# The softmax of the attention given an earlier place in the schedule of a hybrid decoder layer

## The chip, the core and the metric

The kernel runs on one core of a Trainium2 chip. The core has five instruction queues that matter here: TensorE (PE), VectorE (DVE), ScalarE (ACT), GpSimd (POOL) and SyncE (SP), which issues transfers. Each takes its instructions in a fixed order, and an instruction that waits holds all behind it. Times are microseconds on the device, from the start of the program to its end; the median of several runs is the number that counts.

## The reference

The program computes one layer of a decoder on 16 learned tokens and 1024 tokens of width 1024, in 32-bit floats:

```python
u = rmsnorm(h, norm1_w)
rq, rk, rv, rg, dq, dk, dv, gates = split(u @ w_in)
ro = (silu(rg) * group_norm(retention(rope(rq), rope(rk), rv))) @ w_ret_o
dq, dk = rope(rmsnorm(dq)), rope(rmsnorm(dk))
p = softmax(where(mask, q @ k.T / 8, -1e30))     # two maps for each of 8 heads
do = rmsnorm((p[0] - lam * p[1]) @ v) * (1 - lam_init) @ w_diff_o
h = h + (sigmoid(g_ret) * ro + sigmoid(g_diff) * do) @ w_out
a, b = split(causal_dwconv(rmsnorm(h) @ w_up))
out = h + (silu(a) * b) @ w_down
```

The part that the change touches is `p`: the two softmaxes of a head, and their difference with the weight lam.

## The kernel before

Every 32-bit matrix is split into a high part (a cast to fp32r) and a low part (the remainder), and a product is three matmuls: high by high, high by low, low by high. PE therefore streams some 15,000 matmuls, and the other engines cast, subtract, empty the banks and do the rest.

Phase 1 makes the projections of `u` and, among them, the eight heads of attention. `projections` is a generator that gives out half a product (12 matmuls of 342 to 348 columns) at a time; `attention` is another, and `blend` runs the two in turn, 58 units of projection to a head. The finished products go to `evacuate`: for dq and dk it squares them on ACT (L303), splits the squares in sqh (ACT, L241) and sql (DVE, L246), rotates the product on DVE and POOL (L570 to L573), and a little later PE sums the squares by a matmul into the bank `st`. For rq and rk the rotation is L550 to L555, on DVE and POOL as well; for others DVE multiplies once (L606). POOL also computes the low part of the weights (L229).

In `attention`, a block of 128 queries goes through `scores` for both maps. PE makes the scores of a piece of keys into one of four banks `sc` (L175); DVE adds the mask and takes the row's minimum (L686; the scores come negated, so their minimum is the largest logit), which empties the bank; with more than one piece DVE joins the minima (L692); ACT takes the exponential and its sum (L693). When both maps are there, DVE takes the reciprocals (L697) and a product (L698), ACT scales the second map (L699), and DVE adds it to the first (L700). PE then transposes the result (`turn`, L709), ACT and DVE split it in ah and al (L241, L246), and PE multiplies it with the values into the bank `ot`.

The order of the instructions on each engine is fixed when the program is built: outside of a few parts that are ordered by hand, a scheduler takes the instructions by priority, which is their place in the program's text unless something else is said, and by what it estimates to be ready. Tiles come from pools with a few buffers each: two banks `acc` for products, four `sc`, one `st`, one `ot`.

The second to fourth phases (retention, the output products, the MLP) follow and don't call `scores`.

Of the kernel before, what the change touches and what calls it, by code (L numbers as in the profile page):

```python
# [13 lines left out]
AF = mybir.ActivationFunctionType  # L14
ALU = mybir.AluOpType
AX = mybir.AxisListType
# [81 lines left out]
class Builder:  # L98
# [562 lines left out]
    def attention(self, h):  # L661
        V, A, G, E, S = self.V, self.A, self.G, self.E, self.S
# [7 lines left out]
        def scores(t0, m, n, pieces):  # L670

            sm = self.tmp("sm", n=16, bufs=4)
            s = []
            for c in range(2):
                sc_ = self.big() if m > 2 else self.tmp("hs", n=16)
                for i, (a0, sz) in enumerate(pieces):
                    ps = self.sc()
                    self.mm(ps[:m, :sz], QA[c][:, t0:t0 + m], K[c][:, a0:a0 + sz], True, False)
                    self.mm(ps[:m, :sz], QB[c][:, t0:t0 + m], K[c][:, a0:a0 + sz], False, True)
                    if m == 2:  # L680
                        mk = self.hm[:m, :sz]
                    elif i == len(pieces) - 1:
                        mk = self.mask[:, 584 - sz:584]
                    else:
                        mk = self.mask[:, :sz]
                    V.tensor_tensor_reduce(out=sc_[:m, a0:a0 + sz], in0=ps[:m, :sz], in1=mk, scale=1.0, scalar=3e38,  # L686
                                           op0=ALU.add, op1=ALU.min, accum_out=sm[:m, 4 * c + i:4 * c + i + 1])
                np_ = len(pieces)
                mx = sm[:m, 4 * c:4 * c + 1]
                if np_ > 1:  # L690
                    mx = sm[:m, 4 * c + 3:4 * c + 4]
                    V.tensor_reduce(out=mx, in_=sm[:m, 4 * c:4 * c + np_], axis=AX.X, op=ALU.min)  # L692
                A.activation(sc_[:m, :n], sc_[:m, :n], AF.Exp, bias=mx, scale=-1.0,  # L693
                             accum_out=sm[:m, 10 + c:11 + c])
                s.append(sc_)
                yield 0.2 + n / 1000
            V.reciprocal(sm[:m, 12:14], sm[:m, 10:12])  # L697
            V.tensor_mul(sm[:m, 13:14], sm[:m, 13:14], self.nlam[:m])  # L698
            A.activation(s[1][:m, :n], s[1][:m, :n], AF.Copy, scale=sm[:m, 13:14])  # L699
            V.scalar_tensor_tensor(out=s[0][:m, :n], in0=s[0][:m, :n], scalar=sm[:m, 12:13], in1=s[1][:m, :n],  # L700
                                   op0=ALU.mult, op1=ALU.add)
            return s[0]

        def turn(pieces, meta=None):
# [18 lines left out]
        def rows(c):  # L723
            n = NMETA + P * (c + 1)
            k = -(-n // 512)
            sz = [2 * (n // (2 * k))] * k
            sz[0] += n - sum(sz)
            return (yield from scores(NMETA + P * c, P, n, [(sum(sz[:i]), sz[i]) for i in range(k)]))
# [3 lines left out]
        self.spill["do", h] = d, db  # L732
        outs = [(14, 258), (272, 256), (528, 256), (784, 256)]
        halo = yield from scores(HALO, 2, NMETA, [(0, NMETA)])
        ahead = yield from rows(0)

# [4 lines left out]
        for b in range(2):  # L741
            ps = self.tr()
# [5 lines left out]
        ps = self.tr()  # L748
# [4 lines left out]
        for p in range(4):  # L753
# [31 lines left out]
            for jj in range(p + 1):  # L785
# [4 lines left out]
                for kk in range(2):  # L790
                    j = 2 * jj + kk
                    lo = 128 if last and kk == 1 else 0
                    out = ot[:, o0 + lo:nq]
# [6 lines left out]
            t0, n = outs[p]  # L800
# [506 lines left out]
```

## Time and profile before

| | us |
|---|---|
| median of three runs | 2567.45 (2563.02 to 2570.38) |
| profiled execution | 2568.86 |
| its span on the core | 2567.1 |
| TensorE busy | 2509.6 (98%) |
| VectorE busy | 1550.9 (60%) |
| ScalarE busy | 904.0 (35%) |
| GpSimd busy | 816.8 (32%) |

A matmul overlaps the one ahead of it, so busy time of PE is no measure of how fast it goes; the time between the starts of two matmuls is, and where PE idles the trace names the instruction that released it. The granted clock of TensorE is given as a share of 2.4 GHz; half of that, 1.2 GHz, is its other level, and a mean between the two is a stretch in which both occurred. Attention runs from about 100 to 1190 us.

### The profile page before, as it was taken

The page shows a single profiled execution, that of the slowest core. Times are in us where ns is not written, and L with a number is a line of the kernel's source. Part 1 is how long each engine was busy: PE and PEld are TensorE (multiplying, and loading weights), DVE is VectorE, ACT ScalarE, POOL GpSimd, SP SyncE. Part 2 cuts the span into 40 slices and gives each one's busy share as a digit, 9 for nine tenths or more (in the row PEclk, how much of TensorE's full clock was granted, in tenths as well). Part 3 has the DMA queues.
Part 4 walks back from the last instruction along what each step waited for, and adds up shares of the span by engine and source line. Part 5 has one row for each costly group of instructions (what it writes and reads, how often), then busy time and mean ns, then how long its engine had stood idle before and what let it go on. Part 6 is the DMA issues. An engine that isn't in the chain of part 4 may idle for free. (4 is left out here: it accounts for less than half of the span.)

```text
span 2567.1 us, 40420 instructions
## 1 busy us (share of the span) xinstructions
PE 2509.6 (98%) x15444; PEld 2416.9 (94%) x15444; DVE 1550.9 (60%) x3228; ACT 904.0 (35%) x1881; POOL 816.8 (32%) x649
## 2 busy tenths in 40 slices
PE   8999999999999999999999999999999999999999
PEld 8899998999999999999998899999999999999998
DVE  7665757556463737453787887652555566555555
ACT  5343444444343525333466553332311111111111
POOL 1424343322222222222333332434332333333232
PEclk9999999999999999999999999999999999999999
DMA  4524242323324242423443434522111111111112
GB/s 165 129 84 108 63 115 71 107 76 93 104 81 120 62 121 65 117 84 104 116 107 90 105 99 134 185 93 99 38 50 46 50 50 41 50 50 42 50 50 87
DMA packets 171538, 224.55 MB, mean 87 GB/s; under 512 B 26712, under 2 KB 109264, under 8 KB 171344
## 3 DMA queue, kind: packets, MB, share of 16 engines
q1 hardware_dynamic: 165440, 202.70, 26.1%
q0 software_dynamic: 5760, 19.17, 3.5%
q8 instruction: 121, 1.98, 0.3%
q14 instruction: 73, 0.60, 0.1%
q10 hardware_dynamic: 144, 0.10, 0.0%
HBM read 160.20 MB, written 42.35 MB: 79 GB/s over the span
## 5 line engine op out<-in xcount | busy, mean ns | idle before, releaser
L175 PE MATMUL acc<-b,wh 128*128 128x342 f32 (+3 forms) x5948 | 1451.0, 326 | 15.7 <-DVE b L429 9.2
L175 PEld LDWEIGHTS acc<-b,wh 128*128 128x128 f32 x5948 | 1033.7, 190 | 28.4 <-issue 9.2
L175 PE MATMUL acc<-b,wl 128*128 128x342 f32 (+3 forms) x2974 | 966.9, 325 | 1.5 <-POOL wl L229 1.5
L229 POOL TENSOR_TENSOR wl<-wr,wh 128x512 fp32r<-128x512 f32 x366 | 507.6, 1404 | 1148.8 <-ACT wh L228 1136.5
L175 PE MATMUL sc<-b,wh 128*128 128x342 f32 (+2 forms) x2580 | 648.6, 334 | 1.1 <-ACT b L241 1.1
L175 PEld LDWEIGHTS acc<-b,wl 128*128 128x128 f32 x2974 | 564.1, 190 | 7.7 <-POOL wl L229 2.6
L175 PEld LDWEIGHTS sc<-b,wh 128*128 128x128 f32 x2580 | 455.2, 189 | 22.5 <-ACT b L241 1.3
L175 PE MATMUL sc<-b,wl 128*128 128x342 f32 (+2 forms) x1290 | 429.3, 334 | 0.0
L228 ACT CAST wh<-wr 128x512 fp32r<-128x512 f32 x366 | 212.8, 618 | 574.9 <-issue 241.2
L175 PEld LDWEIGHTS sc<-b,wl 128*128 128x128 f32 x1290 | 243.8, 189 | 10.0
L246 POOL TENSOR_TENSOR b<-b,b 128x512 fp32r<-128x512 f32 (+1 forms) x86 | 138.3, 1608 | 304.9 <-ACT b L241 262.7
L606 DVE TENSOR_TENSOR ev<-acc,b 128x342 f32<-128x342 f32 (+1 forms) x144 | 74.0, 514 | 187.7 <-PE acc L175 184.1
L241 ACT CAST b<-b 128x512 fp32r<-128x512 f32 (+3 forms) x137 | 102.1, 750 | 214.0 <-DVE b L1242 145.6
L693 ACT ACTIVATE b<-b,sm 128x272 f32<-128x272 f32 (+7 forms) x128 | 101.0, 789 | 150.4 <-DVE sm L692 118.6
L1205 DVE SCALAR_TENSOR_TENSOR b<-b,cols,b 128x1024 f32<-128x1024 f32 x88 | 148.8, 1691 | 2.3
L686 DVE CUSTOM_DVE_ANT_0 b<-sc,consts 128x144 f32<-128x144 f32 (+6 forms) x224 | 106.6, 503 | 39.3 <-PE sc L175 38.6
L1196 DVE TENSOR_TENSOR b<-sc,b 128x342 f32<-128x342 f32 x84 | 42.5, 511 | 139.4 <-PE sc L175 139.4
L246 DVE TENSOR_TENSOR al<-sc,ah 128x512 fp32r<-128x512 f32 (+2 forms) x144 | 77.6, 539 | 68.3 <-ACT ah L241 68.0
L241 ACT CAST ah<-sc 128x512 fp32r<-128x512 f32 (+2 forms) x144 | 67.3, 467 | 121.8 <-PE sc L709 84.0
L1220 DVE TENSOR_TENSOR b<-b,sc 128x512 f32<-128x512 f32 x117 | 78.7, 683 | 48.8 <-PE sc L175 48.8
L175 PE MATMUL sc<-b,b 128*128 128x264 f32 (+9 forms) x480 | 96.8, 319 | 1.9 <-DVE sm L686 1.9
L1203 DVE TENSOR_SCALAR b<-b,cols 128x1024 f32<-128x1024 f32 x44 | 81.5, 1853 | 1.6
(248 smaller groups left out, 2665.4 us busy)
## 6 DMA issues: line engine op xcount, KB each, us to landing
wr<-w_in SPq DMA_DIRECT2D x170, 256.0 KB
wr<-w_up SPq DMA_DIRECT2D x88, 256.0 KB
d<-ev SPq DMA_DIRECT2D x120, 171.0 KB
b<-b POOLq DMA_DIRECT2D x72, 260.0 KB, 4.6
b<-d SPq DMA_DIRECT2D x256, 64.0 KB
b<-d SPq DMA_DIRECT2D x24, 513.0 KB
wr<-w_down SPq DMA_DIRECT2D x44, 256.0 KB
b<-d SPq DMA_DIRECT2D x32, 260.0 KB
```

Source lines behind the costliest of these rows:

```text
L175: self.E.matmul(out, lhsT=l, rhs=r, start=start, stop=stop)
L228: self.A.copy(h, raw)
L229: (self.G if el == "G" else self.V).tensor_sub(l, raw, h.bitcast(F32))
L241: self.A.copy(dh, src)
L246: (self.V if el == "V" else self.G).tensor_sub(dl, src, dh.bitcast(F32))
L606: V.tensor_mul(o[:, :n], ps[:, :n], self.rb[:, cs])
L686: V.tensor_tensor_reduce(out=sc_[:m, a0:a0 + sz], in0=ps[:m, :sz], in1=mk, scale=1.0, scalar=3e38, op0=ALU.add, op1=ALU.min, accum_out=sm[ ...
L693: A.activation(sc_[:m, :n], sc_[:m, :n], AF.Exp, bias=mx, scale=-1.0, accum_out=sm[:m, 10 + c:11 + c])
L1196: self.V.tensor_mul(up[:, t0:t0 + n], ps[:, :n], self.rb2[:, t0:t0 + n])
L1203: V.tensor_scalar(out=o[:, q], in0=up[:, q], scalar1=self.cw(2, fi), scalar2=self.cb(fi), op0=ALU.mult, op1=ALU.add)
L1205: V.scalar_tensor_tensor(out=o[:, q], in0=up[:, NMETA - 2 + i:T - 2 + i], scalar=self.cw(i, fi), in1=o[:, q], op0=ALU.mult, op1=ALU.add)
L1220: self.V.tensor_add(h, h, ps)
```

## The change

The change puts the operations of `scores` on DVE and ACT under a raised priority: the scheduler takes them as if they stood 300 instructions earlier in the program. No instruction is added, removed or altered. The core of the diff, whose other part puts L692 and L693 under the same line:

```diff
-                    V.tensor_tensor_reduce(out=sc_[:m, a0:a0 + sz], in0=ps[:m, :sz], in1=mk, scale=1.0, scalar=3e38,
-                                           op0=ALU.add, op1=ALU.min, accum_out=sm[:m, 4 * c + i:4 * c + i + 1])
+                    with self.tc.high_priority(offset=300):
+                        V.tensor_tensor_reduce(out=sc_[:m, a0:a0 + sz], in0=ps[:m, :sz], in1=mk, scale=1.0, scalar=3e38,
+                                               op0=ALU.add, op1=ALU.min, accum_out=sm[:m, 4 * c + i:4 * c + i + 1])
...
-            V.reciprocal(sm[:m, 12:14], sm[:m, 10:12])
-            V.tensor_mul(sm[:m, 13:14], sm[:m, 13:14], self.nlam[:m])
-            A.activation(s[1][:m, :n], s[1][:m, :n], AF.Copy, scale=sm[:m, 13:14])
-            V.scalar_tensor_tensor(out=s[0][:m, :n], in0=s[0][:m, :n], scalar=sm[:m, 12:13], in1=s[1][:m, :n],
-                                   op0=ALU.mult, op1=ALU.add)
+            with self.tc.high_priority(offset=300):
+                V.reciprocal(sm[:m, 12:14], sm[:m, 10:12])
+                V.tensor_mul(sm[:m, 13:14], sm[:m, 13:14], self.nlam[:m])
+                A.activation(s[1][:m, :n], s[1][:m, :n], AF.Copy, scale=sm[:m, 13:14])
+                V.scalar_tensor_tensor(out=s[0][:m, :n], in0=s[0][:m, :n], scalar=sm[:m, 12:13], in1=s[1][:m, :n],
+                                       op0=ALU.mult, op1=ALU.add)
```

The lines behind move down by one to three: L686 becomes L687, L692 L694, L697 L700, L698 L701, L700 L703 in the order of the changed kernel. The text goes on by the names of before.

On DVE, in the first block of head 0 (about 125 us in the trace of before), this stood in a row; sh_1193 is the rotated half of a projection, sql_1189 the low half of its squares, sm_1168 the minima and sums of the block, b_1169 its result, b_1235 the next block's scores:

```order
L570 STREAM_SHUFFLE sh_1193<-b_1058 128x346
L246 TENSOR_TENSOR sql_1189<-sq_1187,sqh_1188 128x346
L571 TENSOR_TENSOR b_1058<-b_1058,b_125 128x346
L697 RECIPROCAL sm_1168<-sm_1168 128x2
L573 TENSOR_TENSOR b_1058<-b_1058,sh_1193 128x346
L698 TENSOR_TENSOR sm_1168<-sm_1168,nl 128x1
L686 ISA b_1235,sm_1234<-sc_1236,consts 128x400
L686 ISA sm_1234 128x1
L700 SCALAR_TENSOR_TENSOR b_1169<-b_1169,sm_1168,b_1201 128x272
```

In the changed kernel this stands in its place, on the same engine:

```order
L570 STREAM_SHUFFLE sh_1193<-b_1058 128x346
L700 RECIPROCAL sm_1168<-sm_1168 128x2
L571 TENSOR_TENSOR b_1058<-b_1058,b_125 128x346
L701 TENSOR_TENSOR sm_1168<-sm_1168,nl 128x1
L246 TENSOR_TENSOR sql_1189<-sq_1187,sqh_1188 128x346
L573 TENSOR_TENSOR b_1058<-b_1058,sh_1193 128x346
L687 ISA b_1235,sm_1234<-sc_1236,consts 128x400
L687 ISA sm_1234 128x1
L703 SCALAR_TENSOR_TENSOR b_1169<-b_1169,sm_1168,b_1201 128x272
```

The reciprocal and the product moved ahead by one instruction each and sql_1189 back by three; what stands ahead of the result, L700 of before, is the same set.

On DVE, in a later block of head 2 (about 490 us), where b_5118 holds the scores of one map in three pieces and ev_5107 and x_4949 are a projection's rotation, this stood in a row:

```order
L551 TENSOR_TENSOR ev_5107<-acc_5072,b_127 128x342
L686 ISA b_5118,sm_5117<-sc_5119,consts 128x348
L686 ISA sm_5117 128x1
L554 TENSOR_TENSOR x_4949<-x_4949,b_128 128x342
L686 ISA b_5118,sm_5117<-sc_5123,consts 128x346
L686 ISA sm_5117 128x1
L555 TENSOR_TENSOR ev_5107<-ev_5107,x_4949 128x342
L686 ISA b_5118,sm_5117<-sc_5127,consts 128x346
L686 ISA sm_5117 128x1
```

In the changed kernel the end of the same stretch is this, with the rows of b_5118 ahead of it:

```order
L687 ISA sm_5117 128x1
L551 TENSOR_TENSOR ev_5107<-acc_5072,b_127 128x342
L694 TENSOR_REDUCE sm_5117<-sm_5117 128x1
L554 TENSOR_TENSOR x_4949<-x_4949,b_128 128x342
L555 TENSOR_TENSOR ev_5107<-ev_5107,x_4949 128x342
L687 ISA b_5156,sm_5117<-sc_5157,consts 128x348
```

The three pieces of b_5118 moved ahead of L551 and of the pair L554 and L555, which now stand together.

On DVE, in head 7 (about 1007 us), where sql_10739 is the low half of a projection's squares and b_10632 the result of a block, this stood in a row:

```order
L697 RECIPROCAL sm_10631<-sm_10631 128x2
L698 TENSOR_TENSOR sm_10631<-sm_10631,nl 128x1
L570 STREAM_SHUFFLE sh_10743<-b_10612 128x346
L571 TENSOR_TENSOR b_10612<-b_10612,b_125 128x346
L700 SCALAR_TENSOR_TENSOR b_10632<-b_10632,sm_10631,b_10697 128x656
L246 TENSOR_TENSOR sql_10739<-sq_10737,sqh_10738 128x346
L573 TENSOR_TENSOR b_10612<-b_10612,sh_10743 128x346
```

In the changed kernel it is this:

```order
L700 RECIPROCAL sm_10631<-sm_10631 128x2
L701 TENSOR_TENSOR sm_10631<-sm_10631,nl 128x1
L703 SCALAR_TENSOR_TENSOR b_10632<-b_10632,sm_10631,b_10697 128x656
L570 STREAM_SHUFFLE sh_10743<-b_10612 128x346
L246 TENSOR_TENSOR sql_10739<-sq_10737,sqh_10738 128x346
L571 TENSOR_TENSOR b_10612<-b_10612,b_125 128x346
L573 TENSOR_TENSOR b_10612<-b_10612,sh_10743 128x346
```

The result moved ahead of L570 and L571, and the low half ahead of L571.

## Rows read from the trace of the kernel before

**Rows 1.** The page: busy time of each engine with its share of the span, and the chain that ended last, by engine.

```profile
PE 2509.6 (98%) x15444; PEld 2416.9 (94%) x15444; DVE 1550.9 (60%) x3228; ACT 904.0 (35%) x1881; POOL 816.8 (32%) x649
...
PE 28%; issue 1%; POOL 0%; DVE 0%; POOLq 0%
```

**Rows 2.** Busy time of each engine by stretches of the span: the stretch, its length, PE, weight loads (PEld), DVE, ACT and POOL with their instruction counts, the granted clock of TensorE, the share of the DMA engines, GB/s.

```profile
100.00:230.00 130.00, 123.26 (x790) 121.62 (x789) 80.64 (x194) 56.16 (x130) 46.95 (x45) 0.97 0.34 90
...
1190.00:2567.00 1377.00, 1362.19 (x8064) 1285.47 (x8063) 853.74 (x1564) 416.49 (x799) 467.68 (x323) 1.00 0.27 79
```

**Rows 3.** The waits of PE from 100 to 1190 us: what waited, for what, us in all, times, the longest.

```profile
PE sc L709 <- DVE b L700: 17.9, 13, 3.2
PE ot L175 <- DVE al L246: 3.5, 2, 1.8
PE st L175 <- DVE sql L246: 2.7, 2, 2.5
PE sc L175 <- DVE sm L686: 1.9, 2, 1.3
PE st L175 <- ACT sqh L241: 1.4, 1, 1.4
```

**Rows 4.** The timeline of PE, the first and the last of the six waits in the first block of a head: start, duration, the instruction, and in brackets the idle time before it and what ended it.

```profile
129.46 0.28 PE L709 MATMUL sc<-consts,b 128*16 128x128 f32 x1 [3.22 <-DVE b L700]
...
838.61 0.28 PE L709 MATMUL sc<-consts,b 128*16 128x128 f32 x1 [0.17 <-DVE b L700]
```

**Rows 5.** The timeline of DVE in the first block of head 0, and, last, the rotation's sum in the first block of head 1.

```profile
125.16 0.50 DVE L246 TENSOR_TENSOR sql<-sq,sqh 128x346 fp32r<-128x346 f32 x1
125.58 1.11 DVE L571 TENSOR_TENSOR b<-b,b 128x346 f32<-128x346 f32 x1
...
126.80 1.39 DVE L573 TENSOR_TENSOR b<-b,sh 128x346 f32<-128x346 f32 x1
...
128.91 0.50 DVE L700 SCALAR_TENSOR_TENSOR b<-b,sm,b 128x272 f32<-128x272 f32 x1 [0.16 <-ACT b L699]
...
275.08 0.52 DVE L573 TENSOR_TENSOR b<-b,sh 128x346 f32<-128x346 f32 x1
```

**Rows 6.** The timeline of POOL in the first block of head 0.

```profile
125.42 0.90 POOL L572 TENSOR_TENSOR sh<-sh,b 128x346 f32<-128x346 f32 x1 [0.16 <-DVE sh L570]
126.28 1.53 POOL L229 TENSOR_TENSOR wl<-wr,wh 128x512 fp32r<-128x512 f32 x1
```

**Rows 7.** The timeline of DVE at 492 us.

```profile
492.38 1.58 DVE L554 TENSOR_TENSOR x<-x,b 128x342 f32<-128x342 f32 x1 [1.30 <-POOL ev L552]
493.88 0.51 DVE L686 CUSTOM_DVE_ANT_0 b<-sc,consts 128x346 f32<-128x346 f32 x1
```

**Rows 8.** The timeline of DVE at 440 us.

```profile
439.79 1.44 DVE L246 TENSOR_TENSOR sql<-sq,sqh 128x258 fp32r<-128x258 f32 x1
...
442.70 1.25 DVE L700 SCALAR_TENSOR_TENSOR b<-b,sm,b 128x528 f32<-128x528 f32 x1
443.87 1.59 DVE L554 TENSOR_TENSOR x<-x,b 128x346 f32<-128x346 f32 x1
...
445.94 0.49 DVE L686 CUSTOM_DVE_ANT_0 b<-sc,consts 128x328 f32<-128x328 f32 x1
```

**Rows 9.** The timeline of PE at 440 us, the two places with idle time.

```profile
444.00 0.61 PE L709 MATMUL sc<-consts,b 128*16 128x128 f32 x4 [3.09 <-DVE b L700]
...
446.49 0.64 PE L175 MATMUL sc<-b,b 128*128 128x328 f32 x1 [0.62 <-DVE sm L686]
```

**Rows 10.** The timeline of PE at 1007 us.

```profile
1007.29 0.42 PE L175 MATMUL st<-sqh,constsr 128*128 128x346 f32 x1
1010.20 0.42 PE L175 MATMUL st<-sql,constsr 128*128 128x346 f32 x1 [2.48 <-DVE sql L246]
```

**Rows 11.** The timeline of DVE at 1007 us.

```profile
1005.38 0.17 DVE L697 RECIPROCAL sm<-sm 128x2 f32<-128x2 f32 x1 [1.00 <-ACT b L693]
...
1007.21 1.44 DVE L700 SCALAR_TENSOR_TENSOR b<-b,sm,b 128x656 f32<-128x656 f32 x1
1008.57 1.57 DVE L246 TENSOR_TENSOR sql<-sq,sqh 128x346 fp32r<-128x346 f32 x1
```

**Rows 12.** The waits of PE in three shorter stretches, from 290 to 360 us, from 580 to 612 and from 880 to 890, columns as in the third group.

```profile
PE sc L709 <- DVE b L700: 0.9, 2, 0.5
...
PE sc L709 <- DVE b L700: 0.8, 1, 0.8
...
PE sc L709 <- DVE b L700: 1.8, 1, 1.8
```

**Rows 13.** The timeline of DVE in head 1, a low half of squares.

```profile
262.78 0.50 DVE L246 TENSOR_TENSOR sql<-sq,sqh 128x346 fp32r<-128x346 f32 x1
```

**Rows 14.** The timeline of PE in head 1, the matmul that takes it.

```profile
264.45 0.32 PE L175 MATMUL st<-sql,constsr 128*128 128x346 f32 x1
```

**Rows 15.** Busy time and clock in short stretches behind waits, columns as in the second group.

```profile
126.00:134.00 8.00, 4.78 (x23) 4.40 (x22) 7.68 (x20) 3.02 (x9) 1.81 (x2) 0.81 0.26 89
...
440.00:452.00 12.00, 8.29 (x36) 7.55 (x35) 10.77 (x23) 5.26 (x10) 4.49 (x4) 0.72 0.48 134
562.00:570.00 8.00, 6.43 (x42) 5.96 (x41) 6.42 (x15) 4.17 (x12) 1.93 (x2) 1.00 0.15 44
...
1007.00:1015.00 8.00, 5.52 (x26) 5.06 (x25) 7.53 (x12) 2.19 (x6) 4.29 (x3) 0.79 0.27 87
```

More of the change, by code (lines that the diff above doesn't have):

```diff
@@ L685, in scores @@
                         mk = self.mask[:, :sz]
-                    V.tensor_tensor_reduce(out=sc_[:m, a0:a0 + sz], in0=ps[:m, :sz], in1=mk, scale=1.0, scalar=3e38,
-                                           op0=ALU.add, op1=ALU.min, accum_out=sm[:m, 4 * c + i:4 * c + i + 1])
+                    with self.tc.high_priority(offset=300):
+                        V.tensor_tensor_reduce(out=sc_[:m, a0:a0 + sz], in0=ps[:m, :sz], in1=mk, scale=1.0, scalar=3e38,
+                                               op0=ALU.add, op1=ALU.min, accum_out=sm[:m, 4 * c + i:4 * c + i + 1])
                 np_ = len(pieces)
[L689 to L694, printed above, removed]
+                with self.tc.high_priority(offset=300):
+                    mx = sm[:m, 4 * c:4 * c + 1]
+                    if np_ > 1:
+                        mx = sm[:m, 4 * c + 3:4 * c + 4]
+                        V.tensor_reduce(out=mx, in_=sm[:m, 4 * c:4 * c + np_], axis=AX.X, op=ALU.min)
+                    A.activation(sc_[:m, :n], sc_[:m, :n], AF.Exp, bias=mx, scale=-1.0,
+                                 accum_out=sm[:m, 10 + c:11 + c])
                 s.append(sc_)
                 yield 0.2 + n / 1000
-            V.reciprocal(sm[:m, 12:14], sm[:m, 10:12])
-            V.tensor_mul(sm[:m, 13:14], sm[:m, 13:14], self.nlam[:m])
-            A.activation(s[1][:m, :n], s[1][:m, :n], AF.Copy, scale=sm[:m, 13:14])
-            V.scalar_tensor_tensor(out=s[0][:m, :n], in0=s[0][:m, :n], scalar=sm[:m, 12:13], in1=s[1][:m, :n],
-                                   op0=ALU.mult, op1=ALU.add)
+            with self.tc.high_priority(offset=300):
+                V.reciprocal(sm[:m, 12:14], sm[:m, 10:12])
[3 more added lines that the diff above has]
+                                       op0=ALU.mult, op1=ALU.add)
             return s[0]
```

## The prediction

> **What bounds the kernel now.** I read the page first. TensorE is busy 98% of the span, VectorE 60%, and the chain that ended last has no other engine above 0% [rows 1]. So nothing but PE's idle time, and the time in which its clock is halved, can be won. The stretches by time come next: while attention is interleaved with the projections PE is busy 123.26 of 130 us, with a clock of 0.97; behind 1190 us it is busy 1362 of 1377 us [rows 2]. The changed lines run in the first 1190 us alone, so the waits are read there. PE's waits from 100 to 1190 us [rows 3] name the place: the transposes (L709) waited 13 times, 17.9 us in all, for the weighted difference of the two softmaxes (DVE L700); two waits of 1.9 us are for a score bank that the mask-and-minimum (L686) had not emptied; 2.7 us and 1.4 us are for the squares of the projections (sql, sqh), 3.5 us for the transposed probabilities' low part (al). These are 27.4 us, and every term below is a part of them or of the clock.
>
> **What the change removes and adds.** Nothing: the engines get the same instructions, 3145 on DVE. Of the softmax, DVE's L686, L692, L697, L698, L700 and ACT's L693, L699 get a priority 300 steps earlier, and so DVE's fixed order changes, PE's and ACT's a little. What counts is which DVE instruction stands ahead of the one that PE waits for. I go through the waits.
>
> *First block of a head, six places.* The waits run from 3.22 us (head 0) to 0.17 us (head 5) [rows 4]; with the four between (2.32, 2.22, 1.57 and 0.63) they are 10.1 us. In head 0 PE's transpose stands from 126.2 us. DVE is by then in an unbroken run: L571 1.11 us, L697, L573 1.39, L698, L686, then 0.16 idle, and L700 0.50 us [rows 5]. The new order has the same instructions ahead of L700; L697 and L698 change places with L571 and L573, ACT's L699 can start earlier, and only the 0.16 us of idle time goes: 6 x 0.16 = 1.0 us. In heads 0 and 3 the low half of the squares (L246, sql) also moves behind L571. In before it ran at 125.16 us, its 0.42 us covered while DVE waited for ACT's sum; now it stands in the run: 2 x 0.42 = 0.8 us lost. Where PE waits for sql first and then for L700, that is one wait in two pieces. Bounds: 0.42 lost in all six, -2.5 us; 0.16 won in all six, +1.0. I take +0.2, their sum.
>
> The two long instructions in that run are long because of POOL. L571 starts at 125.58, inside POOL's L572 (125.42, 0.90 us), and L573 at 126.80 inside POOL's 1.53 us cast remainder [rows 6]; with POOL idle the same L573 took 0.52 us, as the last line shows [rows 5]. So the order also decides which instruction meets POOL, and the DVE time ahead of L700 isn't fixed to 0.9 us. The Trainium skill ("SBUF — State Buffer", Who interferes with whom) says that a VectorE instruction with two SBUF inputs contends with a GpSimd instruction that reads SBUF, and that the first to start holds the port until it ends. The trace agrees: L573 ended at 128.19, 0.38 us after POOL's end at 127.81 [rows 5, 6]. By that rule a low half that is moved is held wherever POOL has begun its next instruction, in 46.95 of 130 us here [rows 2], so about one in three; without it, nowhere. It leaves the sum, and is why the slower rival below has 0.15 and not half of it.
>
> *The score bank at 492 us.* DVE had the second L686 of a block behind L554, which stood 1.30 us idle for POOL's L552 and then ran 1.58 us; L686 began at 493.88 [rows 7], and PE waited 1.3 us of the 1.9 of [rows 3]. In the new order all three L686 stand ahead of L551 and L554. Gone: 1.3 us (bounds 0 and 1.3). The evacuation L551 gets later by two L686, 2 x 0.51 = 1.0 us; PE needs that bank only after the next whole product, 24 matmuls, so I cost it at nothing. If that cover were gone it would be 1.0 us.
>
> *Second block of head 2, 440 us.* L700 began at 442.70, behind L246, L550 and L551, and PE stood 3.09 us for it and then 0.62 us for a score bank that L686 emptied from 445.94 on [rows 8, 9]. In the new order L700 stands five rows behind L697, ahead of eight instructions of some 0.5 us that it had to follow before, and PE's order has its transposes pulled 12 matmuls ahead; it should end at about 438, before PE comes. But L686 of the next block (bank sc_4598) now stands behind L551, L554, L264, L555, al and the sql of 1.44 us [rows 8]. DVE was without idle time here, so the eight end at about 442; the five behind L551 take 2.6 us at some 0.5 each, as sql and L700 take alone [rows 5], and 4.6 with L554 at 1.59 and sql at 1.44 [rows 8]. With L686's own 0.5 the bank is free at 445.1 to 447.1, against 446.4 now. PE, which began its wait at 440.9 [rows 9], comes to the product that needs this bank at about 441.4: a wait of 3.7 to 5.7 us under another name, against 3.09 + 0.62 and two restarts of 0.27 (below), 4.2 in all. I take 0, bounds -1.5 and +0.5.
>
> *Head 7, the squares at 1007 us.* PE waited 2.48 us for sql [rows 3, 10], which stood behind L700 of 1.44 us and took 1.57 us itself [rows 11]. In the new order L700 stands ahead of L570 and sql directly behind it, and the L686s ahead of this stand earlier, so that L697's idle 1.00 us for ACT goes. Then sql ends 1.5 to 2.5 us earlier. Gain 1.9 us, bounds 0 and 2.48.
>
> *The rest of the 17.9 us.* 17.9 - 10.1 - 3.1 leaves 4.7. Of these, two (0.8 us at 609, 1.8 us at 884) stand behind multiplications that wait for a transfer or behind ACT's L699, and stay. The other 2.1 us are small ones, as the 0.9 us in two pieces between 290 and 360 us [rows 12]; L700 moves ahead of the pair L554, L555 there. I take 1.4, bounds 0 and 2.1. The 3.5 us for al and the 1.4 for sqh stay.
>
> *Restarts.* The two matmuls around a wait stand further apart than the wait itself: 2.91 us for 2.48 at 1007 [rows 10], and one of these follows the other by 0.16 otherwise, so 0.27 lies in the refill. Some five waits go: about 1.0 us.
>
> *New waits.* In four more places sql moves behind L686 or L571. In head 1 it ended at 263.28 and PE took it at 264.45 [rows 13, 14]: a margin of 1.2 us. Behind L686 (0.29) and L571 (1.11 to 1.25) it is late by up to 0.4 us. Other places have as much margin or more. I take -0.5, bounds 0 and, with sql at 1.57 us as at 1007, 4 x 1.5 = -6.
>
> *The clock.* Behind some waits PE's clock fell: 0.81 granted in the 8 us from 126, 0.72 in the 12 us from 440, 0.79 from 1007, and 1.00 behind the 1.57 us wait at 562 [rows 15]. A granted mean of 0.79 is part of the time at 1.2 GHz instead of 2.4; it loses 0.21 x 8 = 1.7 us, the one at 440 0.28 x 12 = 3.4. With the waits at 126 and 440 still there, those dips stay; the one at 1007 should go, I put 0.8 of it, and 0.1 of the one at 440. I take 1.4 + 0.3 = 1.7, bounds 0 and the 6.6 of these three.
>
> Sum: 0.2 + 1.3 + 0 + 1.9 + 1.4 + 1.0 - 0.5 + 1.7 = 7.0 us. The profiled execution took 2568.86 us (span 2567.1), so 2561.9 on its basis; it lies 1.4 above the median of the runs, 2567.45, and against that it is 2560.5. A measurement of this kernel can tell about 0.3% from no change, 7.7 us: the forecast lies just at that edge.
>
> **Rivals.** *All waits for the softmax go* (0.12). The 17.9 + 1.9 + 2.5 = 22.3 us vanish and with them most of the three dips, some 5: 2540 us. For it: the order is what puts L700 behind the projections' work. Against it: in the six largest places no projection work was passed.
>
> *The waits only change place* (0.22). DVE has the same work ahead of each thing that PE needs, so an earlier L700 means a later evacuation or sql; 0 to 2 us are won, 2566 us. For it: the 440 case. Against it: at 492 and 1007 DVE idled behind POOL and ACT, which the new order fills. The Trainium skill ("Perfetto Trace Analysis", Optimization Strategy) holds that one gap repeating on the engine that should be saturated can mean too few buffers; then order would win nothing, and this rival's time would come. The trace bears it out only for the 1.9 us on score banks; the 17.9 us are waits for data.
>
> *Slower* (0.15). One mechanism: the low half of the squares. PE takes it in a fixed place of the projections' stream, and behind L571 it is 1.11 us late and, meeting POOL, 1.07 longer (1.57 against 0.50). In six places that is 6 x 2.2 = 13 us, and with a dip behind each (1.5) 9 more, less the 7.0 won: 2582.5 us. It decides where the delay is above the margin of 1.2 us by more than 1 us. Against it: only sql of head 0 has no margin, and there PE stood for L700 anyway.
>
> **How the numbers follow.** The forecast has 0.51, with a range of its own from 2554 to 2566. Faster by over 0.3% (below 2559.8): 0.24 of it, all of the first rival, 0.04 of the second: 0.40. Slower (above 2575.1): 0.13 of the third, 0.02 of the second: 0.15. Within: 0.45. The range from 2549 to 2573 leaves out most of the first and of the third rival.
>
> **What would show it.** Right: PE's waits for sc from DVE L686 fall from 1.9 to below 1 us, the 2.5 us at 1007 to below 1, with a clock of 1.00 behind it; L700's waits fall from 17.9 to about 15, with the first blocks still there; the 440 wait bears the name of L686 instead of L700. Wrong: waits of st for sql above 4 us in all, first-block waits below 5 us, or the last 1377 us changed by more than 1 us.

## The result, and the profile after

The changed kernel takes 2548.36 us (median of four runs, 2544.51 to 2549.88), the kernel before beside it 2567.59: a ratio of 0.9925, 95% interval 0.9906 to 0.9943, or 19.2 us less. The forecast was 7.0 us less. The time lies just below the range (2549 to 2573). The profiled execution took 2549.15 us with a span of 2547.4, 19.7 below the span before; the rest of this section goes by the two profiled executions.

The page of the changed kernel, busy time of each engine, answers to [rows 1]:

```profile
PE 2499.9 (98%) x15444; PEld 2410.9 (95%) x15444; DVE 1542.3 (61%) x3228; ACT 903.9 (35%) x1881; POOL 817.3 (32%) x649
```

The shares tell nothing here: PE stays at 98% and the others move by a point at most. The waits of PE from 100 to 1190 us, columns as in [rows 3], tell more. The transposes are L712 and the weighted difference is L703 by the changed kernel's numbers:

```profile
PE sc L712 <- DVE b L703: 10.8, 9, 2.8
PE sc L175 <- DVE am L264: 1.8, 1, 1.8
PE ot L175 <- DVE al L246: 1.6, 1, 1.6
PE st L175 <- ACT sqh L241: 1.4, 1, 1.4
PE st L175 <- DVE sql L246: 0.2, 1, 0.2
```

They sum to 15.8 us, 11.6 less than the 27.4 of [rows 3], in 13 waits and not 20. The waits for a score bank (1.9) are gone, those for sql fell from 2.7 to 0.2, and those for the result of the softmax from 17.9 to 10.8. Most of the last comes from what the prediction calls the first block of a head. (The result that PE waits for there, 128x272, is that of the second block, of 272 keys: PE transposes the blocks in pairs, and this ends the first pair. The block at 440 us, of 528 keys, likewise ends the second pair.) In the timeline of PE, the waits of heads 0, 1 and 3 that answer to [rows 4] are:

```profile
126.69 0.28 PE L712 MATMUL sc<-consts,b 128*16 128x128 f32 x1 [1.88 <-DVE b L703]
...
269.71 0.28 PE L712 MATMUL sc<-consts,b 128*16 128x128 f32 x1 [0.79 <-DVE b L703]
...
544.95 0.28 PE L712 MATMUL sc<-consts,b 128*16 128x128 f32 x1 [1.07 <-DVE b L703]
```

Head 2 has none now, nor has head 4; head 5 has 0.16. The six were 10.1 us and are 3.9. Of the waits that are left, the longest is new, at 727 us:

```profile
729.75 1.10 PE L712 MATMUL sc<-consts,b 128*16 128x128 f32 x5 [2.83 <-DVE b L703]
```

The clock is the second half of the gain. In the kernel before, a granted clock of 0.79 in 8 us stands at 217, 274 and 415 us too, beside the three places of [rows 15]. In these rows of the kernel before the columns are as in [rows 2]:

```profile
217.00:225.00 8.00, 6.19 (x32) 5.99 (x30) 4.79 (x7) 1.03 (x2) 4.30 (x6) 0.79 0.53 122
274.00:282.00 8.00, 5.68 (x28) 5.21 (x28) 6.31 (x14) 4.33 (x11) 4.07 (x4) 0.79 0.12 33
415.00:423.00 8.00, 5.78 (x29) 5.19 (x28) 6.68 (x17) 3.88 (x11) 1.61 (x2) 0.79 0.00 0
```

Part of each stretch ran at 1.2 GHz. With the loss worked out as in the prediction, (1 - clock) x length, the six places cost 1.5 + 3.4 + 4 x 1.7 = 11.7 us. After, in the same view:

```profile
123.00:131.00 8.00, 6.12 (x40) 5.55 (x39) 7.83 (x20) 4.20 (x11) 2.35 (x2) 1.00 0.28 89
248.00:256.00 8.00, 8.00 (x46) 7.83 (x47) 5.89 (x21) 3.54 (x14) 3.08 (x4) 0.79 0.00 0
427.00:435.00 8.00, 6.16 (x30) 5.95 (x29) 6.02 (x19) 2.43 (x6) 3.77 (x3) 0.79 0.55 175
727.00:735.00 8.00, 5.25 (x24) 5.05 (x25) 6.67 (x15) 5.28 (x11) 2.68 (x2) 0.79 0.11 36
1007.00:1015.00 8.00, 7.49 (x51) 7.49 (x51) 5.37 (x12) 4.56 (x9) 0.00 (x0) 1.00 0.17 55
```

Three stretches of 1.7 us are left, 5.1 us: 6.6 less, in one execution of each kernel. The account is then 11.6 (waits) + 6.6 (clock) + 1.9 (seven fewer restarts of 0.27, the figure of the prediction) = 20.1 us, against 19.7 measured.

### The profile page after: what moved, and what is told of

Same layout as the page of the kernel before. It is cut to its first block, busy times and chain, and to the rows that moved or that the text cites. A ratio compares the mean times of both kernels' runs of the same rounds, so it can differ in the third digit from the quotient of the medians.

```text
span 2547.4 us, 40419 instructions
## 1 busy us (share of the span) xinstructions
PE 2499.9 (98%) x15444; PEld 2410.9 (95%) x15444; DVE 1542.3 (61%) x3228; ACT 903.9 (35%) x1881; POOL 817.3 (32%) x649
## 3 DMA queue, kind: packets, MB, share of 16 engines
q8 instruction: 121, 1.98, 0.3%
## 5 line engine op out<-in xcount | busy, mean ns | idle before, releaser
L229 POOL TENSOR_TENSOR wl<-wr,wh 128x512 fp32r<-128x512 f32 x366 | 506.6, 1401 | 1150.4 <-ACT wh L228 1147.6
L687 DVE CUSTOM_DVE_ANT_0 b<-sc,consts 128x144 f32<-128x144 f32 (+6 forms) x224 | 105.7, 504 | 42.1 <-PE sc L175 41.4
```

Of the source, the lines that this page charges most:

```text
L229: (self.G if el == "G" else self.V).tensor_sub(l, raw, h.bitcast(F32))
```

## The experiments

What had to be explained was the first blocks, for which the prediction allowed 0.16 us each. In head 2 the wait fell from 2.22 us to nothing. The run of DVE ahead of the result is the same set of instructions, but it begins earlier. In the kernel before, ACT and DVE show this ahead of that run; first ACT:

```profile
412.40 0.52 ACT L693 ACTIVATE b<-b,sm 128x272 f32<-128x272 f32 x1 [2.58 <-DVE sm L686]
...
412.92 0.44 ACT L303 ACTIVATE sq<-acc 128x348 f32<-128x348 f32 x1
413.26 0.54 ACT L569 ACTIVATE b<-acc,qkw 128x348 f32<-128x348 f32 x1
```

and DVE, in the kernel before:

```profile
410.47 1.09 DVE L573 TENSOR_TENSOR b<-b,sh 128x346 f32<-128x346 f32 x1
411.60 0.28 DVE L264 TENSOR_TENSOR vm<-sc,vm 16x128 fp32r<-16x128 f32 x1
411.91 0.44 DVE L686 CUSTOM_DVE_ANT_0 b<-sc,consts 128x272 f32<-128x272 f32 x1
...
413.84 0.56 DVE L570 STREAM_SHUFFLE sh<-b 128x348 f32<-128x348 f32 x1
```

The exponential L693 stands at the head of ACT's queue and waits 2.58 us for the minimum that L686 gives. Behind it stand the projection's square L303 and its copy L569, and DVE's rotation L570, which is the head of the run, waits for L569. So L686, behind L573 and L264 on DVE, sets when the run begins. After the change, on ACT:

```profile
399.84 0.52 ACT L695 ACTIVATE b<-b,sm 128x272 f32<-128x272 f32 x1 [1.11 <-DVE sm L687]
...
400.36 0.44 ACT L303 ACTIVATE sq<-acc 128x348 f32<-128x348 f32 x1
400.70 0.54 ACT L569 ACTIVATE b<-acc,qkw 128x348 f32<-128x348 f32 x1
```

and on DVE:

```profile
399.37 0.42 DVE L687 CUSTOM_DVE_ANT_0 b<-sc,consts 128x272 f32<-128x272 f32 x1
...
399.73 0.74 DVE L573 TENSOR_TENSOR b<-b,sh 128x346 f32<-128x346 f32 x1
400.50 0.28 DVE L264 TENSOR_TENSOR vm<-sc,vm 16x128 fp32r<-16x128 f32 x1
...
401.29 0.56 DVE L570 STREAM_SHUFFLE sh<-b 128x348 f32<-128x348 f32 x1
```

L686 (now L687) stands ahead of L573. The theory, A, was this chain: an earlier L686 frees ACT sooner, and with ACT the projection's work that DVE's run begins with. The rival was that the run itself is shortened by the earlier tail (L697 to L700). A second question was which blocks give the gain: the small ones (up to 144 keys: two queries on the 16 learned tokens, and the first 128 queries of a head) or the others, to which the block of 272 keys belongs. In the expectations of the first four runs the rival is called B, and A stands for the softmax of the small blocks. Medians are given with those of the kernel before that ran on the same chip beside them.

**The small blocks alone.** Against the changed kernel, at all three places:

```diff
-                    with self.tc.high_priority(offset=300):
+                    with self.tc.high_priority(offset=300) if n <= 144 else nullcontext():
```

> Only the halo's and the first query block's softmax (at most 144 keys, two calls a head) gets the raised priority; 30 rows of difference on DVE, none on PE. Theory A (the first-block waits shrank because the small softmaxes ahead of them, whose steps go from DVE to ACT and back, end sooner, so that ACT comes sooner to the projection's L303 and L569 and DVE's run of L570 to L700 starts sooner): PE's six first-block waits for L700 fall from 10.1 us to 4 to 6, some of the clock dips behind them go, and the waits at 440 (3.1), 492 (1.3) and 1007 us (2.5) stay; 2557 to 2561 us. Theory B (they shrank because L697, L698, L699 and L700 of the block itself were put ahead): first-block waits stay at 9 to 10 us, 2565 to 2568 us.

2563.19 against 2567.35 us, 0.9987 (0.9979 to 0.9996). The first-block waits are still 9.0 us (B had 9 to 10), though the time fits neither theory; those at 440 (3.43), 492 (1.29) and 1007 (2.47) stay. So the small blocks give 1 to 5 us by the interval, and most of the gain is not theirs. In its profile what they give stands in the clock: PE's waits in attention sum to 27.9 us, no less than before, but three stretches of 1.7 us are left (behind 126, 274 and 1003 us). At 440 the wait is there and the slow stretch isn't, as the row of this kernel that answers to [rows 15] shows:

```profile
440.00:452.00 12.00, 10.92 (x73) 10.64 (x74) 8.67 (x22) 5.25 (x12) 1.23 (x1) 1.00 0.52 146
```

**The other blocks alone.** The same with `n > 144`.

> The complement: the raised priority for all softmax blocks but the halo and the first. Theory A: first-block waits stay at 8 to 10 us; the score-bank wait at 492 and the squares' wait at 1007 are gone and the new wait of 2.8 us at 727 is there; 2556 to 2561 us, and the gains of this and of the run with the halo and first block alone add up to that of the whole change (about 19 us). Theory B: first-block waits at 4 us as in the changed kernel, 2548 to 2551 us.

2545.17 against 2567.35 us, 0.9919 (0.9905 to 0.9932): as much as the whole change. The six first-block waits are 3.6 us, where theory A had 8 to 10 and B 4, so A in the form it had then, by the small blocks, is refuted. All L703 waits are:

```profile
PE sc L712 <- DVE b L703: 7.3, 7, 2.0
```

The small blocks' part of the change isn't needed. It can cost: in the changed kernel, ACT in head 1 shows L702 of a small block (L699 of before) at the head of its queue,

```profile
259.29 0.41 ACT L702 ACTIVATE b<-b,sm 128x144 f32<-128x144 f32 x1 [2.45 <-DVE sm L701]
...
260.08 0.46 ACT L303 ACTIVATE sq<-acc 128x348 f32<-128x348 f32 x1
```

and L303 of the projection behind it: theory A's chain with the sign turned round.

**The mask-and-minimum alone.** Against the kernel before, L686 under the raised priority and nothing else:

```diff
-                    V.tensor_tensor_reduce(out=sc_[:m, a0:a0 + sz], in0=ps[:m, :sz], in1=mk, scale=1.0, scalar=3e38,
+                    with self.tc.high_priority(offset=300):
+                        V.tensor_tensor_reduce(out=sc_[:m, a0:a0 + sz], in0=ps[:m, :sz], in1=mk, scale=1.0, scalar=3e38,
```

> Only L686 (mask and minimum) gets the raised priority. Theory A: first-block waits 4 to 6 us, since it is L686 of the small softmaxes that stood behind L571 or L573; the wait at 492 gone; the squares at 1007 still waited for at 1.5 us or more, since L700 still stands ahead of sql; 2554 to 2559 us. Theory B: first-block waits 9 us or more; 2561 to 2566 us.

2555.26 against 2567.35 us, 0.9961 (0.9949 to 0.9974): 12 us. The wait at 492 is gone and 1.54 us are left for sql at 1007, as expected. The six first-block waits are 7.2 us, though, between the 4 to 6 of theory A and the 9 of B: heads 3 and 5 rose, from 1.57 to 1.82 and from 0.17 to 0.83. In the timeline of PE in head 2 the wait of 2.22 us is nearly gone:

```profile
411.62 0.28 PE L710 MATMUL sc<-consts,b 128*16 128x128 f32 x1 [0.19 <-DVE b L701]
```

**The tail alone.** L697 to L700 under the raised priority, the rest as before.

> Only L697, L698, L699 and L700 get the raised priority. Theory A: first-block waits 8 to 10 us, the wait at 492 stays at 1.3 us, the one at 1007 falls below 1.5 us; 2560 to 2566 us. Theory B: first-block waits 5 us or less; 2552 to 2557 us.

2559.84 against 2567.35 us, 0.9971 (0.9961 to 0.9981). The first blocks keep 9.2 of 10.1 us, where B had 5 or less, and what is won lies elsewhere: the 3.09 us at 440 fell to 1.05, with 1.84 for am (L264) behind it. Head 2 shows:

```profile
410.84 0.28 PE L710 MATMUL sc<-consts,b 128*16 128x128 f32 x1 [1.91 <-DVE b L701]
```

The 2.48 us at 1007, which I had expected to fall below 1.5, stayed: there the result keeps its place behind L571 as long as the steps ahead of it aren't earlier.

**The exponential alone.** L692 and L693 under the raised priority.

> Only L692 and L693 (joined minimum, exponential) get the raised priority; L686, L697 to L700 stay. If the first-block waits follow the place of L686 on DVE (L693 of the block waits for it at the head of ACT's queue, the projection's L303 and L569 behind it, DVE's L570 behind these), L570 starts where it starts in the kernel before (19.8, 17.6, 20.1, 18.9 and 19.0 us behind the same PE instruction in heads 0 to 4) to within 0.2 us, and the first-block waits stay at 9 to 10 us, less what a half-clock stretch in front of one takes; 2563 to 2568 us. If it is ACT's own order that counts, L570 starts 0.5 us earlier or more in at least three heads, and 2555 to 2561 us.

2566.43 against 2565.88 us, 1.0004 (0.9995 to 1.0013): nothing. It is a weak test of ACT's own order, since raising these two alone hardly moves it: in head 2 ACT takes the same instructions in the same order as before, and its exponential waits 2.57 us for L686 (2.58 before). PE's wait there is the full one:

```profile
418.92 0.28 PE L710 MATMUL sc<-consts,b 128*16 128x128 f32 x1 [2.21 <-DVE b L701]
```

In head 1, L570 came 0.7 us later than before; I had expected it within 0.2.

**Minimum and exponential, without the tail.** The changed kernel with L697 to L700 as before.

> L686, L692 and L693 raised, L697 to L700 not. If the start of L570 is set by L686 and the length of the run to L700 by the tail, L570 starts where it does in the changed kernel (18.5, 17.9, 18.0, 18.5, 18.2 us in heads 0 to 4, to within 0.5) and the run from L570 to L700 takes what it takes in the kernel before (3.45 us in heads 1, 2 and 4, 4.2 in 0 and 3), 0.3 more than in the changed one in heads 1, 2 and 4; the wait at 1007 stays above 1.5 us; 2551 to 2557 us. If the tail also sets the start, L570 starts as in the kernel before.

2552.77 against 2565.88 us, 0.9949 (0.9936 to 0.9961). This and the tail give 13.1 + 7.5 = 20.6 us, the whole change 19.2 (20.9 in its second timing): in time the two parts add up within the intervals. In the first blocks they don't: 7.6 us of waits are left here, 2.6 less than before, and the tail alone took 0.9. The wait at 1007 was gone, where I had expected 1.5 us or more. Built this way, the order has L700 ahead of L570 and sql directly behind it without any priority on L700; that the scheduler reckons its inputs ready earlier is my guess. The run in heads 0 and 3, which I had expected at 4.2 us, took 5.36.

From the timelines of these kernels, the start of the L570 that heads the run of a first block, in us after the start of one matmul of PE that stands ahead of it (the same in every kernel); then the time from L570 to the start of the result in heads 0 and 3, and the six first-block waits together:

| | head 0 | 1 | 2 | 3 | 4 | run, heads 0, 3 | six waits |
|---|---|---|---|---|---|---|---|
| before | 19.77 | 17.57 | 20.05 | 18.92 | 19.01 | 4.19, 4.22 | 10.1 |
| minimum alone | 18.46 | 17.36 | 18.01 | 18.47 | 18.20 | 5.19, 5.20 | 7.2 |
| minimum and exponential | 18.46 | 17.84 | 18.02 | 18.47 | 18.19 | 5.36, 5.36 | 7.6 |
| exponential alone | 19.77 | 18.29 | 20.04 | 18.91 | 19.01 | 4.36, 4.38 | 9.4 |
| tail alone | 19.77 | 17.57 | 20.03 | 18.89 | 19.00 | 4.20, 4.23 | 9.2 |
| whole change | 18.47 | 17.87 | 18.02 | 18.46 | 18.17 | 4.14, 4.15 | 3.9 |
| other blocks alone | 19.33 | 17.16 | 18.59 | 18.45 | 18.17 | 4.13, 4.15 | 3.6 |
| small blocks alone | 18.90 | 18.28 | 19.49 | 18.92 | 19.01 | 4.20, 4.23 | 9.0 |

Kernels with L686 raised everywhere start L570 between 0.45 and 2.04 us earlier in heads 0, 2, 3 and 4; with the exponential alone or the tail alone it stays there, within 0.03 us. From the minimum of the block's first map to L570 it is 1.91 to 1.98 us in heads 1, 2 and 4 and 2.43 to 2.45 in heads 0 and 3, in each of these kernels: the minimum does set the start. The run from L570 to the result in head 2 is 3.47 us before and in every kernel without the tail, and 3.16 where the tail of these blocks is raised: the rival is worth 0.3 us there, theory A 2.0. Head 1 goes the other way with the small blocks raised, as its ACT rows showed.

In heads 0 and 3 the earlier start alone isn't enough. With the minimum raised and the tail not, the product L698 (here L700) falls behind L686 of the next block, and the result stands for ACT's L699 (here L701), as DVE in head 0 of the kernel with minimum and exponential shows:

```profile
126.12 0.15 DVE L700 TENSOR_TENSOR sm<-sm,nl 128x1 f32<-128x1 f32 x1
...
127.40 0.50 DVE L702 SCALAR_TENSOR_TENSOR b<-b,sm,b 128x272 f32<-128x272 f32 x1 [0.70 <-ACT b L701]
```

The run grows by 1.0 to 1.2 us, which takes back most of the earlier start in head 0 and more than that in head 3. With the tail raised as well it is 4.15 us again. So theory A explains head 2 (and head 4); in heads 0 and 3 it takes the minimum and the tail together, which neither A nor the rival had said.

**Before and after, once more.** Both kernels unaltered, on one chip.

> The kernel before once more, for a second profile. If PE's half-clock stretches are tied to the waits in front of them, between 100 and 1190 us there are again six or seven of 1.7 us lost each, at the same places (behind 126, 217, 276, 417, 440, 1007 us); if they fall by chance, other places and 3 to 7 of them. The waits themselves (18 of over 0.25 us) come again to within 0.1 us either way, except where a stretch at half clock lies ahead of one: PE then comes later and waits less, by up to 1.7 us.

> The changed kernel once more, on the chip of the next two runs and for a second profile. 2546 to 2550 us. If the half-clock stretches are tied to waits: 3 between 100 and 1190 us, as in the first profile, behind 247, 427 and 727 us; if by chance, anything from 2 to 6, and the first-block wait of head 1 (0.79 us behind a half-clock stretch at 248) is 2.0 to 2.5 us when none lies ahead of it.

One execution of the kernel before took 2568.75 us; the changed kernel 2547.08 against 2567.99, 0.9919 (0.9905 to 0.9933). Its three stretches at a lower clock stood at 248, 427 and 727 us again. In the kernel before, four places came again; the one at 217 was missing, and one had moved, from 274 to 252 us. So it loses 10.0 us where the first execution lost 11.7, and of the 6.6 us that the clock gave above, 1.7 hang on which execution is taken. The moved one, as this execution shows,

```profile
252.00:260.00 8.00, 6.40 (x32) 5.71 (x31) 7.17 (x19) 2.85 (x9) 2.14 (x2) 0.79 0.03 11
276.00:284.00 8.00, 7.19 (x48) 6.91 (x47) 5.72 (x16) 5.50 (x15) 3.50 (x3) 1.00 0.21 66
```

lay ahead of the wait of head 1, which was 0.81 us and not 2.32, with the same order of instructions: PE reached it 20.80 us after that fixed matmul and not 19.26. Where the stretch at 217 was missing, a wait stood that the first execution doesn't have:

```profile
225.74 0.38 PE L175 MATMUL ot<-al,vh 128*128 128x256 f32 x1 [1.28 <-DVE al L246]
```

The other waits came again to within 0.1 us, but for 0.2 more at 446 and 0.4 more at 885. Head 1's transpose began 21.58 us after the fixed matmul in the first execution, 21.60 in this one and 21.57 in the changed kernel. So the fall of head 1 from 2.32 to 0.79 us is no gain of the change; PE only came later, behind a slow stretch. Of the 6.2 us won in the first blocks about 4.7 are left to the change. From the fixed matmul to the transpose, summed over heads 0 to 4, the whole change is 5.4 us ahead of the kernel before, the minimum and the exponential alone 2.1, the tail alone 1.0: some 2.3 us come only with both.

**What is left, 1.** At 727 us the timeline of DVE in the changed kernel shows where the new wait comes from:

```profile
723.30 1.25 DVE L593 TENSOR_TENSOR b<-b,b 128x1040 f32<-128x1040 f32 x1 [4.62 <-DMA b<-d]
...
728.66 1.03 DVE L703 SCALAR_TENSOR_TENSOR b<-b,sm,b 128x784 f32<-128x784 f32 x1 [0.34 <-ACT b L702]
```

DVE stands 4.62 us for the norm's row, which is stored and read back through memory (L590 issues the reading); the softmax is queued behind it. To the kernel with the other blocks alone, the norm's operations, its store and its reading back are added under the same priority:

```diff
-                    y = self.rstat(st, 348, eps=self.eps)
+                    with self.tc.high_priority(offset=300):
+                        y = self.rstat(st, 348, eps=self.eps)
...
-                for r in (0, 64):
+                with self.tc.high_priority(offset=300):
+                    for r in (0, 64):
```

> As the run without the halo and first block, and with the raised priority also for the projections' norm (the square root's chain in evacuate's stat and its transfers, L278 to L282, L584, L590). Theory: the wait at 727 us (2.83 us in the changed kernel, 2.02 in that run) comes from DVE standing at L593 for a broadcast that starts late because the softmax passed the norm's chain; then it is below 0.5 us here, and the median 1 to 4 us below that run's 2545. Rival: L593's transfer is late for the SyncE queue's own order; then the wait stays at 2 us and the median at 2545 to 2548.

2543.9 against 2567.99 us, 0.9905 (0.9892 to 0.9919). The wait at 727, 2.02 us in the kernel that this is built on, fell to 1.3 us, not below 0.5:

```profile
PE sc L714 <- DVE b L705: 1.3, 1, 1.3
```

DVE (L593 and L700 are L595 and L705 here) stood 3.02 us for the row (3.84 in the kernel that this is built on), and the result then another 1.92 for ACT's L699, where it had 0.34:

```profile
719.29 1.24 DVE L595 TENSOR_TENSOR b<-b,b 128x1040 f32<-128x1040 f32 x1 [3.02 <-DMA b<-d]
...
726.50 1.04 DVE L705 SCALAR_TENSOR_TENSOR b<-b,sm,b 128x784 f32<-128x784 f32 x1 [1.92 <-ACT b L704]
```

So the theory was right in part at most. The rival isn't settled, because the edit raises the norm's operations and its transfers at once, and the gain in time isn't shown: the ratios of the two kernels overlap.

**What is left, 2.** The same kernel with the split of the transposed probabilities in `turn` raised instead:

```diff
-                self.stack(meta[:, :n], ps[:rows, :n], second="l")
+                with self.tc.high_priority(offset=300):
+                    self.stack(meta[:, :n], ps[:rows, :n], second="l")
```

(and `split` of the other rows in the same way)

> As the run without the halo and first block, and with the raised priority also for what empties the banks of the transposes (L241, L246 and L264 of turn). Theory: the wait of 1.8 us at 427, where PE stands for a bank that L264 empties behind L551, L554 goes, and so do the 1.6 us at 185 for al: 2 to 5 us below that run. Rival: the same DVE work stands in front of another bank or of L700 then, and the median stays within 1.5 us of it.

2543.71 against 2567.99 us, 0.9905 (0.989 to 0.992). At 427 us one wait went from 1.85 to 1.3; the one for al (1.6) stays, and the one at 727 is 2.8 us, where the kernel that this is built on has 2.02. The median lies 1.46 us below that kernel's, within the rival's 1.5, and the ratios overlap: no gain is shown.

**Both.**

> The two additions together: no raise for the halo and first block, the norm's chain and the emptying of the transposes' banks raised. If their gains are independent (1.3 and 1.5 us against the run without them) the median is 2541 to 2543 us; if they share the DVE time in the same places, 2543 to 2545.

2540.79 us (2538.83 to 2544.03) against 2565.88, 0.9908 (0.9893 to 0.9923). It has the lowest median of all, but it ran on another chip than the changed kernel, and the ratios overlap: that it is faster than the changed kernel isn't shown. Its profile has no stretch at the lower clock in attention: taken in stretches of 10 us from 100 to 1190, each of the 109 rows shows 1.00, as this one does (columns as in [rows 2]):

```profile
1000.00:1010.00 10.00, 8.50 (x58) 8.22 (x56) 7.08 (x13) 4.38 (x8) 0.00 (x0) 1.00 0.35 107
```

## Why the prediction was wrong

The direction and the kind of gain were right, and the size was less than half. By its terms (the waits of the first profiled execution of each kernel; the stretches at the lower clock and the restarts are worked out as above):

| term | forecast | measured |
|---|---|---|
| first blocks | +0.2 | +6.2 (10.1 to 3.9; 1.5 of it no gain, head 1) |
| score bank at 492 | +1.3 | +1.3 |
| second block of head 2 | 0 | +1.9 (3.09 + 0.62 to 1.84) |
| squares at 1007 | +1.9 | +2.5 |
| the rest of L700's waits | +1.4 | -2.2 (4.7 to 6.9) |
| waits for al, "stay" | 0 | +1.9 (3.5 to 1.6) |
| restarts | +1.0 | +1.9 (seven, worked out) |
| new waits for sql | -0.5 | 0 |
| clock | +1.7 | +6.6 |

**First blocks: "only the 0.16 us of idle time goes".** This step failed. It compared what stands between L570 and the result, and took the start of L570 as given. That start follows L686 through ACT's queue, and L686 did move: L570 began 0.46 to 2.03 us earlier in heads 0, 2, 3 and 4. Nor was the length of the run safe: it stays at 4.15 us in heads 0 and 3 only because the tail is raised too, and is 5.2 to 5.4 without. About 4.7 us were won in place of 0.2. The row that would have said so, ACT's 2.58 us behind L686, was in the trace of before; I had read DVE's and POOL's rows there and not ACT's. The sentence against the first rival, "in the six largest places no projection work was passed", fell with it: in head 2 L686 did pass L573, ahead of the part that I had looked at.

The terms inside the run came out as a wash, 4.19 us in head 0 before and 4.14 after, though not as the prediction reckoned. It charged 0.42 us for the low half sql, taken as covered in the kernel before; but there sql stands in the same unbroken run, between L570 and L571 [rows 5]. The timeline of DVE in the changed kernel has

```profile
122.59 0.52 DVE L571 TENSOR_TENSOR b<-b,b 128x346 f32<-128x346 f32 x1
123.03 0.76 DVE L701 TENSOR_TENSOR sm<-sm,nl 128x1 f32<-128x1 f32 x1
123.71 0.51 DVE L246 TENSOR_TENSOR sql<-sq,sqh 128x346 fp32r<-128x346 f32 x1
124.14 1.58 DVE L573 TENSOR_TENSOR b<-b,sh 128x346 f32<-128x346 f32 x1
```

with POOL, in the same kernel,

```profile
122.70 1.07 POOL L572 TENSOR_TENSOR sh<-sh,b 128x346 f32<-128x346 f32 x1 [0.17 <-DVE sm L700]
123.73 1.61 POOL L229 TENSOR_TENSOR wl<-wr,wh 128x512 fp32r<-128x512 f32 x1
```

L571 began 0.11 us ahead of POOL's L572 and took 0.52 us, where it began inside it before and took 1.11 [rows 5]; L573 again began inside the remainder L229 and ended 0.38 us behind it. What L571 won, the small product L701 lost: it began inside L572, ended 0.02 us behind it and took 0.76 us, where L698 of before took 0.15. The Trainium skill ("SBUF — State Buffer", Who interferes with whom) has the engine that starts first hold the port; L571 at 0.52 and 1.11 us agrees in both directions.

**492 and 1007** came out by their steps. At 1007 the whole 2.48 went, and sql is met without idle time; a part that the prediction hadn't counted is that L700 and sql took 0.91 and 0.50 us there and not 1.44 and 1.57. **440**: the wait did change its name, but not to L686. What PE's score product waits for is a bank that had held transposes and that L264 (am) empties, 1.84 us. The estimate of 3.7 to 5.7 us took all eight instructions as an unbroken row ahead of L686; the measured wait is below its lower end.

**The rest and the new waits.** The small ones went, as counted; the prediction looked for new waits at sql and had none for the result itself. Three came or grew: 2.83 at 727, 1.96 at 591 (0.82 before, at 609), 1.29 at 1007 (0.47 before, at 1028). The first stands behind a transfer that was hidden, not behind DVE's work. **The al waits, "stay"**: one at 217 went. The gap of DVE's L554 there, which waits for POOL's L552, fell from 3.43 to 2.17 us. I did not test why.

**The clock: "those dips stay".** This step failed as well, and not only through the first. In the changed kernel the wait in head 0 is 1.88 us and the clock behind it 1.00, with 3.22 it was 0.81; but a shorter wait isn't shown to be the reason. With the other blocks alone 1.87 us had 0.79 behind it (8 us from 126), the same wait with the transposes' split raised 1.00, and with the small blocks alone the 3.43 us at 440 had 1.00. What puts a stretch at the lower clock behind one wait and not another stays open. The three stretches at 217, 274 and 415 were not in the sum at all, for I had asked for the clock only at the waits that I meant to move. The two failed terms, first blocks and clock, are 6.0 + 4.9 = 10.9 us of the 12.2 us between forecast (7.0) and measurement (19.2); 1.5 us of the first and 1.7 of the second hang on where the slow stretches fell in one execution.

The rival "all waits for the softmax go" (2540 us) came closer than the forecast, though 10.8 us of its waits remain. "The waits only change place" holds for 440 and 727. The slower one, by the low half, shows nowhere: sql waits are 0.2 us. Of the signs that the prediction named, the waits for L700 fell to 10.8 us and not to about 15, and the first blocks to 3.9, below the 5 that it gave as a sign of being wrong. Its 3145 instructions on DVE are on no row; the page has 3228 for both kernels.

## What to carry to other kernels

When an instruction is moved, follow what it releases through the other engine's queue: one that waits at the head of a queue holds work of another chain, and that work may be the start of the run which the bound engine waits for. Read the run ahead of a wait back to what set its start before calling its length fixed, and list every stretch at the lower clock, not those beside the waits in question. Here the minimum, which releases others, gave 12 us when raised alone, the tail 7.5 and the exponential, which only waits for the minimum, nothing; an operation raised to the head of a queue where it then waits can hold what is behind it, as ACT's 2.45 us in head 1 shows.

## What was unexpected of the hardware

A stretch at 1.2 GHz ahead of a wait takes most of the wait away: the same kernel showed 2.32 us of waiting with the slow stretch behind it and 0.81 with one of 1.7 us ahead, and the matmul that waited began at the same time to 0.02 us (21.58 and 21.60 us after the fixed one). At 226 us it was the other way round: 1.28 us of waiting came where the slow stretch ahead was missing. So single waits differ by 1.5 us between executions of one kernel, and a wait that vanishes is no proof of a gain.

Waits of nearly one length had either clock behind them. In the changed kernel 1.84 us at 427 was followed by 0.79, 1.96 us at 591 by 1.00 (8 us from 589), and 1.88 us at 126 by 1.00; the kernel with both additions, whose longest wait in attention is 1.9 us, showed none below 1.00. With the small blocks alone 3.43 us was followed by 1.00, where 3.09 in the kernel before had 0.72. Six places in one execution before and five in another, three after, three with the small blocks alone though its waits sum to as much as before, and none with both additions: the loss went from 11.7 us to nothing, but that fewer waits are what takes it away isn't shown.
